# A two-layer transformer on one Trainium2 core: the experts' routing in program order, its rows by halves, the first gather inside the first expert

## The chip, the cores and the metric

One NeuronCore of a Trainium2 chip runs the kernel; the other seven idle. Its engines are TensorE (PE), VectorE (DVE), ScalarE (ACT), GpSimd (POOL) and SyncE (SP), each with an instruction queue of its own, and 16 DMA engines. The metric is the device time of one execution in microseconds, lower is better.

## The reference, cut to what matters

The model has two blocks of two layers on a sequence of 256 positions with 1024 features, batch 1. What the change touches is the last sublayer, a mixture of eight experts of which each position uses two:

```python
def _moe(h, w_router, w_gu, w_down):
    hf = h.reshape(B * S, D)
    probs = jax.nn.softmax((hf @ w_router).astype(jnp.float32), axis=-1)
    vals, idx = lax.top_k(probs, TOP_K)
    wts = vals / jnp.sum(vals, axis=-1, keepdims=True)
    combine = jnp.sum(jax.nn.one_hot(idx, N_EXPERTS, dtype=jnp.float32) * wts[..., None], axis=1)
    y = jnp.zeros_like(hf)
    for e in range(N_EXPERTS):
        y = y + combine[:, e:e + 1] * _swiglu(hf, w_gu[e], w_down[e])
    return y.reshape(B, S, D)
```

Here h is the normalized and modulated residual (rmsnorm(x) * (1 + scale) + shift), and _swiglu multiplies silu(gate) with up and projects back from 1792 to 1024.

## The kernel before, in words

The 256 positions stand as two halves t of 128 partitions. All of the model is float32: every matrix product is made of three TensorE passes over a high and a low part (hi, lo) of each operand. Weights are streamed by the class Stream: SyncE loads a raw tile, ScalarE casts it to whi (L98), VectorE subtracts to get wlo (L99), and six pairs of buffers hold what is split. Stream.next hands out the next pair and splits ahead until five are in hand; its argument hold leaves that many out. In out_proj, the last projection before the experts, hold grows towards the end (more=2), so that only one pair of the experts' weights is split when it ends. W.behind holds the next twelve splits back behind two given instructions.

Instructions are ordered on each engine by the framework's scheduler, which may run a later one first. Inside the context manager in_order(PE, SC, V) each instruction of TensorE, ScalarE and VectorE is tied to the one traced before it on its engine, so that these three run in program order. In the kernel before, only run() stands inside it: the experts. The routing ahead of it is left to the scheduler.

The routing, from L1212 on: route(t) (L1195) transposes a half of xres in two groups of four blocks, copies each to SBUF on ScalarE, and multiplies by the router's weights wr; eight rows of logits lie in PSUM, are copied to lgT (L1206), transposed back (L1236) and scaled by the norm rs[t] with a bias (L1237). The square root of the norm is ScalarE's (L507 in rsqrt). VectorE takes maximum and index (L1244, L1245), makes the one-hot sel of the two chosen experts (L1246 to L1250), and three small matmuls count each position's slot in its expert, posm (L1252 to L1255). Meanwhile norm_rows makes the modulated rows h (L551 on VectorE, L553 on GpSimd or VectorE), split into hr: the high part on ScalarE (L1261), the low part on GpSimd or VectorE (L1262). Then come the token weights w (L1267 to L1278), the largest count over (L1284), and the weights wj and the row numbers ij by which the experts' results are collected at the end (L1294 to L1303).

experts() makes gather(e0) for each pair of experts: four selection matrices Sm on VectorE (L1343), and eight steps block(c), each four matmuls of 256 columns (L1352) and two casts to xT on ScalarE (L1356). run() calls all eight blocks of the first pair ahead of the first expert, then goes through eight experts e, each in four quarters j of 448 columns, each quarter in eight pieces i: st.next, and six matmuls (L1467 to L1469). A quarter's gate half goes through Silu on ScalarE (L1471), its up half is multiplied on VectorE (L1474), and the quarter before is turned and multiplied by the down weights in the same stretch. For the later pairs the gather's steps are already dealt out one by one inside the pieces:

```python
            def run():
                steps = gather(0)
                for _ in range(KD):
                    steps.pop(0)()
```

Of the kernel before, what the change touches and what calls it, by code (L numbers as in the profile page):

```python
# [11 lines left out]
I32 = mybir.dt.int32  # L12
# [176 lines left out]
def model(ctx: ExitStack, tc: tile.TileContext, A, out, cap=128):  # L189
# [355 lines left out]
    def norm_rows(t, scale, shift=None, r=None):  # L545
# [8 lines left out]
        return h  # L554

# [636 lines left out]

    def route(t):
# [12 lines left out]
        V.tensor_copy(lgT[t], pr[0:8, 0:128])  # L1206
# [5 lines left out]
    with moe_ph as ph:  # L1212
        hr = [po.tile([128, 2, D], F32R, name=x) for x in ("oh", "ol")]
        unit = p.tile([128, 2, 144], F32R, name="unit")
        V.tensor_copy(unit[:, :, 0:128], ident[:, None, :].to_broadcast([128, 2, 128]))
        posm = p.tile([128, 2, 8], F32, name="posm")
        over = p.tile([128, 1], I32, name="over")
        slot = p.tile([128, 2, 128], F32, name="slot")
        for i in range(2):
            GP.iota(slot[:, i], pattern=[[1, 128]], base=i * cap + 1, channel_multiplier=0,  # L1220
                    allow_small_or_imprecise_dtypes=True)
            if cap < 128:
                GP.memset(slot[:, i, cap:], -5.0)
        p0 = p
        tri = p.tile([128, 128], F32R, name="tri")
        V.tensor_scalar(tri, jp, 0.0, None, op0=OP.is_gt)
        io8 = p.tile([128, 8], F32, name="io8")
        GP.iota(io8, pattern=[[1, 8]], base=0, channel_multiplier=0, allow_small_or_imprecise_dtypes=True)
        sel = p.tile([128, 2, 8], F32R, name="sel")
        lg = p.tile([128, 2, 8], F32, name="lg")  # L1230
        pl = pc()
        rs = []
        for t in range(2):
            route(t)
            rs.append(norm_r(t))
            PE.transpose(pl[:, t * 8:t * 8 + 8], lgT[t], ident[0:8, 0:8])  # L1236
            V.scalar_tensor_tensor(lg[:, t], pl[:, t * 8:t * 8 + 8], rs[t], bias8, op0=OP.mult, op1=OP.add)  # L1237
        warm(AF.Exp)
# [4 lines left out]
        for t in range(2):  # L1243
            V.max(top[:, t], lg[:, t])  # L1244
            V.max_index(ti[:, t], top[:, t], lg[:, t])  # L1245
        V.tensor_copy(tf, ti[:, :, 0:2])  # L1246
        oh = p.tile([128, 2, 2, 8], F32, name="oh2")
        V.tensor_tensor(oh, io8[:, None, None, :].to_broadcast([128, 2, 2, 8]),
                        tf[:, :, :, None].to_broadcast([128, 2, 2, 8]), OP.is_equal)
        V.tensor_add(sel, oh[:, :, 0], oh[:, :, 1])  # L1250
        ps = pc()
        PE.matmul(ps[:, 0:8], lhsT=tri, rhs=sel[:, 0], start=True, stop=True)  # L1252
        PE.matmul(ps[:, 8:16], lhsT=ones, rhs=sel[:, 0], start=True, stop=False)
        PE.matmul(ps[:, 8:16], lhsT=tri, rhs=sel[:, 1], start=False, stop=True)
        V.scalar_tensor_tensor(posm, ps[:, 0:16].rearrange("p (t e) -> p t e", t=2), 1.0, sel.bitcast(F32),  # L1255
                               op0=OP.add, op1=OP.mult)
        for t in range(2):
            h = norm_rows(t, *mo_rows, r=rs[t])
            for j in range(2):
                sl = slice(j * 512, (j + 1) * 512)  # L1260
                fs = SC.copy(hr[0][:, t, sl], h[:, sl])  # L1261
                fv = (GP if (t, j) in ((0, 0), (0, 1), (1, 1)) else V).tensor_sub(hr[1][:, t, sl], h[:, sl], hr[0][:, t, sl].bitcast(F32))  # L1262
        W.behind(fs, fv)

        pr = p.tile([128, 2, 8], F32, name="pr")
        sums = p.tile([128, 2], F32, name="sums")
        V.tensor_sub(pr, lg, b3(top[:, :, 0]))  # L1267
        SC.activation(pr, pr, AF.Exp)
        V.tensor_reduce(sums, pr, axis=AX.X, op=OP.add)
        V.reciprocal(sums, sums)  # L1270
        V.tensor_mul(pr, pr, b3(sums))
# [274 lines left out]
```

## Time and profile before

| | us |
|---|---|
| median of 3 runs | 1327.18 |
| lowest, highest | 1326.76, 1331.44 |
| the profiled execution's own time | 1326.26 |
| its span, first to last instruction | 1324.4 |
| TensorE busy | 1254.7 (95%) |
| VectorE busy | 1076.9 (81%) |
| ScalarE busy | 846.5 (64%) |
| GpSimd busy | 37.0 (3%) |

All other numbers come from that one execution. "Busy" adds up the intervals in which an engine had an instruction running; TensorE's weight loads (PEld) overlap its matmuls. The granted clock (PEclk) is a share of 2.4 GHz, so 1.00 is 2.4 GHz and 0.50 is 1.2 GHz. In a timeline, a row stands for one instruction or for neighbours of one kind (x8), with the start of the first and the time from there to the end of the last; in brackets stands how long the engine had been idle before, and what ended that.

### The profile page before, as it was taken

How to read it: one execution, taken by the hardware profiler on the slowest of the kernel's cores; microseconds unless marked ns; L12 is line 12 of the kernel's file. 1: busy time of each engine (PE TensorE's matmuls, PEld its weight loads, DVE VectorE, ACT ScalarE, POOL GpSimd, SP SyncE). 2: the span in 40 equal slices, each digit the busy share in tenths (PEclk: the TensorE clock that was granted, in tenths of full speed). 3: DMA queues.
4: the chain of work that ended last, by engine and by line, in shares of the span. 5: the costliest groups of instructions: out<-in, count | busy, mean ns of one | idle time of the engine just before them, and what ended most of it. 6: DMA issues, size and time to landing. Idle time of an engine off the chain costs nothing. (4 is left out here: it accounts for less than half of the span.)

```text
span 1324.4 us, 20099 instructions
## 1 busy us (share of the span) xinstructions
PE 1254.7 (95%) x7459; PEld 1118.0 (84%) x7459; DVE 1076.9 (81%) x1761; ACT 846.5 (64%) x1354; POOL 37.0 (3%) x68
## 2 busy tenths in 40 slices
PE   6988999999999989999998988999999999999985
PEld 6976989999798779999987667899999889988873
DVE  6796799997897496878768867988888898888976
ACT  7874456555566453434447747788778777878762
POOL 4000000000100000000000020000000000000100
PEclk9988999999899989999979998999999999999987
DMA  9844599892785287899642145999999999999980
GB/s 330 305 143 148 159 384 343 295 315 96 231 259 163 80 307 262 312 382 346 221 138 92 32 138 192 389 372 361 368 385 366 352 381 363 370 357 391 375 320 34
DMA packets 190171, 359.56 MB, mean 271 GB/s; under 512 B 15460, under 2 KB 147970, under 8 KB 189937
## 3 DMA queue, kind: packets, MB, share of 16 engines
q1 hardware_dynamic: 187361, 351.70, 75.1%
q10 hardware_dynamic: 1584, 3.91, 0.8%
q0 software_dynamic: 1120, 2.58, 0.5%
q8 instruction: 61, 1.00, 0.3%
q14 instruction: 45, 0.37, 0.1%
HBM read 351.56 MB, written 7.06 MB: 271 GB/s over the span
## 5 line engine op out<-in xcount | busy, mean ns | idle before, releaser
L99 DVE TENSOR_TENSOR wlo<-raw,whi 128x1024 fp32r<-128x1024 f32 (+2 forms) x577 | 644.5, 1155 | 126.0 <-ACT whi L98 119.0
L98 ACT CAST whi<-raw 128x1024 fp32r<-128x1024 f32 (+2 forms) x577 | 557.7, 1003 | 115.9 <-PE pa L489 30.8
L1467 PE MATMUL pa<-whi,xT 128*128 128x448 f32 x512 | 189.3, 370 | 3.8 <-ACT whi L98 3.8
L1468 PE MATMUL pa<-wlo,xT 128*128 128x448 f32 x512 | 187.0, 365 | 1.7 <-DVE wlo L99 1.7
L1469 PE MATMUL pa<-whi,xT 128*128 128x448 f32 x512 | 186.0, 363 | 0.0
L289 DVE SCALAR_TENSOR_TENSOR acc<-raw,cact,acc 128x1024 f32<-128x1024 f32 x84 | 107.2, 1276 | 2.9 <-DMA raw<-in_w_ada_dram 2.7
L1467 PEld LDWEIGHTS pa<-whi,xT 128*128 128x128 f32 x512 | 96.7, 189 | 11.9 <-ACT whi L98 4.9
L1468 PEld LDWEIGHTS pa<-wlo,xT 128*128 128x128 f32 x512 | 96.8, 189 | 9.4 <-DVE wlo L99 3.1
L1469 PEld LDWEIGHTS pa<-whi,xT 128*128 128x128 f32 x512 | 96.5, 189 | 6.4
L486 PE MATMUL pb<-whi,hTh 128*128 128x512 f32 x224 | 88.4, 395 | 0.7 <-ACT hTh L524 0.7
L487 PE MATMUL pb<-wlo,hTh 128*128 128x512 f32 x224 | 88.4, 395 | 0.1
L478 PE MATMUL pb<-hTh,whi 128*128 128x256 f32 x512 | 74.6, 289 | 1.1 <-ACT hTh L575 0.9
L478 PEld LDWEIGHTS pb<-hTh,whi 128*128 128x128 f32 x512 | 70.3, 196 | 6.0 <-ACT hTh L575 1.6
L478 PE MATMUL pb<-hTl,whi 128*128 128x256 f32 x512 | 72.4, 283 | 0.0
L478 PE MATMUL pb<-hTh,wlo 128*128 128x256 f32 x512 | 71.9, 283 | 0.0
L489 PE MATMUL pb<-whi,hTl 128*128 128x512 f32 x224 | 71.0, 395 | 0.0
L487 PE MATMUL pa<-wlo,fh 128*128 128x512 f32 x176 | 69.2, 393 | 0.6 <-DVE wlo L99 0.6
L486 PE MATMUL pa<-whi,fh 128*128 128x512 f32 x176 | 69.3, 394 | 0.0
L478 PEld LDWEIGHTS pb<-hTl,whi 128*128 128x128 f32 x512 | 66.3, 192 | 0.0
L478 PEld LDWEIGHTS pb<-hTh,wlo 128*128 128x128 f32 x512 | 66.1, 192 | 0.0
L478 PE MATMUL pc<-hTh,whi 128*128 128x256 f32 x448 | 63.8, 285 | 1.2 <-ACT whi L98 1.2
L478 PE MATMUL pc<-hTh,wlo 128*128 128x256 f32 x448 | 63.0, 283 | 0.0
(433 smaller groups left out, 2074.0 us busy)
## 6 DMA issues: line engine op xcount, KB each, us to landing
raw<-in_moe_w_gu_dram SPq DMA_DIRECT2D x128, 896.0 KB, 7.4
raw<-in_moe_w_down_dram SPq DMA_DIRECT2D x56, 1024.0 KB, 6.7
raw<-in_w_ada_dram SPq DMA_DIRECT2D x48, 1024.0 KB, 7.8
raw<-in_w_up_dram SPq DMA_DIRECT2D x22, 1024.0 KB, 9.7
raw<-in_ffn_w_gu_dram SPq DMA_DIRECT2D x22, 1024.0 KB, 6.2
raw<-in_na_w_qkv_dram SPq DMA_DIRECT2D x12, 1024.0 KB, 5.1
raw<-in_w_down_dram SPq DMA_DIRECT2D x11, 1024.0 KB, 4.8
raw<-in_ffn_w_down_dram SPq DMA_DIRECT2D x11, 1024.0 KB
```

What stands on the lines that cost most here:

```text
L98: self.last = self.nc.scalar.copy(h, src)
L99: self.nc.vector.tensor_sub(l, src, h.bitcast(F32))
L289: V.scalar_tensor_tensor(ada_acc[0], raw, cact[:, k:k + 1], ada_acc[0], op0=OP.mult, op1=OP.add)
L478: PE.matmul(ps, lhsT=w[:, k], rhs=x[:, k], start=n + k == 0, stop=n == 2 and k == KD - 1)
L486: PE.matmul(acc[t][j][:, :n], lhsT=xh, rhs=ws[j][0], start=first, stop=False)
L487: PE.matmul(acc[t][j][:, :n], lhsT=xh, rhs=ws[j][1], start=False, stop=False)
L489: PE.matmul(acc[t][j][:, :n], lhsT=xl, rhs=ws[j][0], start=False, stop=last)
L1467: PE.matmul(ps, lhsT=xh, rhs=wh, start=k == 0, stop=False)
L1468: PE.matmul(ps, lhsT=xh, rhs=wl, start=False, stop=False)
L1469: PE.matmul(ps, lhsT=xl, rhs=wh, start=False, stop=k == KD - 1)
```

## The change

The routing moves into run()'s program order: a new function routing(gather) issues it, given to experts as first. Its order is written out by hand: half 0's norm, router, first half row and logits, then half 1's, then the choice, then the other half rows. The rows are made by halves of 512 columns, row (two VectorE instructions), head (ScalarE) and rest (VectorE); GpSimd has no part in them any more, and W.behind goes. route(t) hands back its last copy so that routing can place it. keep_clock(n) issues n matmuls of 512 columns on constants. Only gather(0)'s four Sm are made in routing; its eight blocks are dealt out two by two to the first four pieces of the first expert, behind st.next. The token weights, over, wj and ij move to weigh(), which is called once, at the first piece of the first expert's second quarter (j = 1, i = 0). The switch of ScalarE's table to Exp ahead of the routing's end (warm) goes. The constants unit, tri, io8 and slot are issued ahead of out_proj. Cut to its core:

```diff
+
+    def keep_clock(n):
+
+        ps = pbc()
+        for _ in range(n):
+            tc.keep_in_program_order(PE.matmul(ps, lhsT=ones, rhs=ones[:, None, :].to_broadcast([128, 4, 128]),
+                                               start=True, stop=True))
...
+    unit = p.tile([128, 2, 144], F32R, name="unit")
+    V.tensor_copy(unit[:, :, 0:128], ident[:, None, :].to_broadcast([128, 2, 128]))
...
+    tri = p.tile([128, 128], F32R, name="tri")
+    V.tensor_scalar(tri, jp, 0.0, None, op0=OP.is_gt)
+    io8 = p.tile([128, 8], F32, name="io8")
+    GP.iota(io8, pattern=[[1, 8]], base=0, channel_multiplier=0, allow_small_or_imprecise_dtypes=True)
...
                 PE.matmul(pr[0:8, 0:128], lhsT=wr[:, k], rhs=xT[:, j], start=k == 0, stop=k == KD - 1)
-        V.tensor_copy(lgT[t], pr[0:8, 0:128])
+        return lambda: V.tensor_copy(lgT[t], pr[0:8, 0:128])
...
-        W.behind(fs, fv)
...
+        hx = [wk.tile([128, D], F32, name="h") for _ in range(2)]
+        pl = pc()
+        rs = []
+
+        def logits(t):
+            PE.transpose(pl[:, t * 8:t * 8 + 8], lgT[t], ident[0:8, 0:8])
...
+        def row(t, j):
+            sl = slice(j * 512, (j + 1) * 512)
+            V.scalar_tensor_tensor(hx[t][:, sl], xres[:, t, sl], rs[t], mo_rows[0][:, sl], op0=OP.mult, op1=OP.mult)
+            V.tensor_add(hx[t][:, sl], hx[t][:, sl], mo_rows[1][:, sl])
+        def head(t, j):
+            sl = slice(j * 512, (j + 1) * 512)
+            SC.copy(hr[0][:, t, sl], hx[t][:, sl])
+        def rest(t, j):
+            sl = slice(j * 512, (j + 1) * 512)
+            V.tensor_sub(hr[1][:, t, sl], hx[t][:, sl], hr[0][:, t, sl].bitcast(F32))
+        def choose():
+            V.tensor_copy(tf, ti[:, :, 0:2])
+            V.tensor_tensor(oh, io8[:, None, None, :].to_broadcast([128, 2, 2, 8]),
+                            tf[:, :, :, None].to_broadcast([128, 2, 2, 8]), OP.is_equal)
+            V.tensor_add(sel, oh[:, :, 0], oh[:, :, 1])
+            ps = pc()
+            PE.matmul(ps[:, 0:8], lhsT=tri, rhs=sel[:, 0], start=True, stop=True)
+            PE.matmul(ps[:, 8:16], lhsT=ones, rhs=sel[:, 0], start=True, stop=False)
+            PE.matmul(ps[:, 8:16], lhsT=tri, rhs=sel[:, 1], start=False, stop=True)
+            V.scalar_tensor_tensor(posm, ps[:, 0:16].rearrange("p (t e) -> p t e", t=2), 1.0, sel.bitcast(F32),
+                                   op0=OP.add, op1=OP.mult)
+        def weigh():
+            V.tensor_sub(pr, lg, b3(top[:, :, 0]))
+            SC.activation(pr, pr, AF.Exp)
+            V.tensor_reduce(sums, pr, axis=AX.X, op=OP.add)
+            V.reciprocal(sums, sums)
...
+            ps = pc()
+            for t in range(2):
+                PE.matmul(ps[:, 0:8], lhsT=ones, rhs=sel[:, t], start=t == 0, stop=t == 1)
+            V.tensor_reduce(cnt, ps[:, 0:8], axis=AX.X, op=OP.max)
+            V.tensor_copy(over, cnt)
+            tmp4 = ssx["junk"][:, 0:32].rearrange("p (t j e) -> p t j e", t=2, j=2)
...
+            V.tensor_mul(tmp4, oh, b4(w))
...
+            V.tensor_copy(ij, pj)
+        def routing(gather):
+
+            rs.append(norm_r(0))
+            copy = route(0)
+            row(0, 0)
+            copy()
+            logits(0)
+            row(0, 1)
+            rs.append(norm_r(1))
+            copy = route(1)
             for j in range(2):
+                head(0, j)
+            copy()
+            logits(1)
+            keep_clock(4)
+            choose()
+            row(1, 0)
+            head(1, 0)
+            steps = gather(0)
+            rest(0, 0)
+            rest(1, 0)
+            row(1, 1)
+            head(1, 1)
+            rest(0, 1)
+            rest(1, 1)
+            keep_clock(8)
+            return steps
 
...
             def run():
-                steps = gather(0)
-                for _ in range(KD):
-                    steps.pop(0)()
+                steps = first(gather) if first else gather(0)
                 prev, fin, when = None, None, {}
...
                             w = st.next(hold=2 if e == 7 and j == 3 and i > 4 else 0)
-                            if steps and i % 2 == 0:
+                            if e == j == 0 and i < 4:
                                 steps.pop(0)()
+                                steps.pop(0)()
+                            elif steps and i % 2 == 0:
+                                steps.pop(0)()
+                            if gate is not None and (e, j, i) == (0, 1, 0):
+                                weigh()
...
-        experts(W, slot[:, 0], last_gate)
+        experts(W, slot[:, 0], last_gate, first=routing)
```

## Rows read from the trace of the kernel before

**Rows 1.** Busy time by stretch: us, PE, PEld, DVE, ACT, POOL, clock, DMA share, GB/s

```profile
760.00:780.00 20.00, 20.00 (x97) 15.46 (x97) 7.09 (x14) 7.18 (x14) 0.65 (x3) 1.00 0.56 184
789.00:794.00 5.00, 0.28 (x2) 0.13 (x1) 4.93 (x8) 1.72 (x5) 3.40 (x3) 1.00 0.20 58
794.50:804.00 9.50, 5.82 (x23) 5.32 (x24) 5.54 (x33) 3.03 (x10) 1.29 (x1) 0.50 0.03 9
809.40:1255.00 445.60, 445.60 (x2225) 401.79 (x2226) 392.48 (x411) 360.14 (x464) 1.62 (x1) 1.00 1.02 370
```

**Rows 2.** TensorE's groups of instructions while the experts run: busy, mean | idle

```profile
L1467 PE MATMUL pa<-whi,xT 128*128 128x448 f32 x480 | 176.5, 368 | 0.4 <-ACT whi L98 0.4
```

**Rows 3.** Timeline of PE in the routing: start, us, engine, line, operation [idle before]

```profile
782.69 1.03 PE L1200 MATMUL pb<-ident,xres 128*128 128x128 f32 x8
783.96 1.92 PE L1205 MATMUL pc<-acc,wr 128*8 128x128 f32 x16 [0.24 <-ACT acc L1202]
...
792.19 0.22 PE L1236 MATMUL pc<-ident,shiftl 8*128 8x8 f32 x1 [3.14 <-DVE shiftl L1206]
796.96 0.38 PE L1252 MATMUL pc<-sel,tri 128*128 128x8 f32 x1 [4.55 <-DVE sel L1250]
...
799.41 0.93 PE L1352 MATMUL pc<-Sm,oh 128*128 128x256 f32 x2 [1.22 <-DVE unit L1277]
...
805.39 0.50 PE L1352 MATMUL pc<-Sm,oh 128*128 128x256 f32 x2 [0.27 <-ACT xT L1356]
...
806.50 0.36 PE L1467 MATMUL pa<-whi,xT 128*128 128x448 f32 x1
806.70 0.36 PE L1468 MATMUL pa<-wlo,xT 128*128 128x448 f32 x1
...
809.37 0.47 PE L1468 MATMUL pa<-wlo,xT 128*128 128x448 f32 x1 [0.65 <-DVE wlo L99]
```

**Rows 4.** Timeline of POOL in the routing

```profile
789.93 3.13 POOL L1262 TENSOR_TENSOR ol<-h,oh 128x512 fp32r<-128x512 f32 x2 [0.65 <-ACT oh L1261]
```

**Rows 5.** Timeline of DVE in the routing

```profile
785.26 0.75 DVE L551 SCALAR_TENSOR_TENSOR h<-xres,ry,bc 128x512 f32<-128x512 f32 x1
...
789.52 2.42 DVE L551 SCALAR_TENSOR_TENSOR h<-xres,ry,bc 128x512 f32<-128x512 f32 x2
...
793.53 0.21 DVE L1237 SCALAR_TENSOR_TENSOR lg<-pc,ry,bias 128x8 f32<-128x8 f32 x1
793.67 0.68 DVE L553 TENSOR_TENSOR h<-h,bc 128x512 f32<-128x512 f32 x1
...
796.75 0.16 DVE L1250 TENSOR_TENSOR sel<-oh 128x16 fp32r<-128x16 f32 x1
...
797.80 0.18 DVE L1255 SCALAR_TENSOR_TENSOR posm<-pc,sel 128x16 f32<-128x16 f32 x1 [0.57 <-PE pc L1254]
...
799.36 0.28 DVE L1343 TENSOR_SCALAR Sm<-slot,posm 128x128 fp32r<-128x128 f32 x1
...
800.96 0.17 DVE L1303 CAST ij<-junk 128x4 int32<-128x4 f32 x1
808.23 4.10 DVE L99 TENSOR_TENSOR wlo<-raw,whi 128x896 fp32r<-128x896 f32 x4 [7.10 <-ACT whi L98]
```

**Rows 6.** Timeline of ACT in the routing

```profile
783.33 1.07 ACT L1202 COPY acc<-pb 128x512 f32<-128x512 f32 x2 [1.02 <-PE pb L1200]
...
786.98 0.29 ACT L507 ACTIVATE ry<-ssx,re 128x1 f32<-128x1 f32 x1
...
804.69 1.20 ACT L1356 CAST xT<-pc 128x256 fp32r<-128x256 f32 x4 [0.42 <-PE pc L1352]
...
807.24 5.16 ACT L98 CAST whi<-raw 128x896 fp32r<-128x896 f32 x6
```

**Rows 7.** Timeline of all engines at the first expert's first quarters

```profile
813.25 1.28 ACT L1471 ACT_TABLE_LOAD   x1
...
819.97 0.61 DVE L1474 TENSOR_TENSOR hm<-hm,pa 128x448 f32<-128x448 f32 x1
```

More of the change, by code (lines that the diff above doesn't have):

```diff
@@ L1191, in model @@
     lgT = [sh.tile([KD, 128], F32, name="shift" + x) for x in "hl"]
+    unit = p.tile([128, 2, 144], F32R, name="unit")
+    V.tensor_copy(unit[:, :, 0:128], ident[:, None, :].to_broadcast([128, 2, 128]))
+    posm = p.tile([128, 2, 8], F32, name="posm")
+    over = p.tile([128, 1], I32, name="over")
+    slot = p.tile([128, 2, 128], F32, name="slot")
+    for i in range(2):
+        GP.iota(slot[:, i], pattern=[[1, 128]], base=i * cap + 1, channel_multiplier=0,
+                allow_small_or_imprecise_dtypes=True)
+        if cap < 128:
+            GP.memset(slot[:, i, cap:], -5.0)
+    tri = p.tile([128, 128], F32R, name="tri")
+    V.tensor_scalar(tri, jp, 0.0, None, op0=OP.is_gt)
+    io8 = p.tile([128, 8], F32, name="io8")
+    GP.iota(io8, pattern=[[1, 8]], base=0, channel_multiplier=0, allow_small_or_imprecise_dtypes=True)
     def route(t):
@@ L1213, in model @@
         hr = [po.tile([128, 2, D], F32R, name=x) for x in ("oh", "ol")]
[L1214 to L1228, printed above, removed]
         sel = p.tile([128, 2, 8], F32R, name="sel")
         lg = p.tile([128, 2, 8], F32, name="lg")
[L1231 to L1238, printed above, removed]
         b3 = lambda x, n=8: x[:, :, None].to_broadcast([128, 2, n])
@@ L1242, in model @@
         tf = p.tile([128, 2, 2], F32, name="tf")
-        for t in range(2):
+        oh = p.tile([128, 2, 2, 8], F32, name="oh2")
+        pr = p.tile([128, 2, 8], F32, name="pr")
+        sums = p.tile([128, 2], F32, name="sums")
+        w = p.tile([128, 2, 8], F32, name="w")
+        cnt = p.tile([128, 1], F32, name="cnt")
+        wj = p.tile([128, 2, 2], F32, name="wj")
+        ij = p.tile([128, 2, 2], I32, name="ij")
+        hx = [wk.tile([128, D], F32, name="h") for _ in range(2)]
+        pl = pc()
@@ L1250, in model @@
[L1250 to L1258, printed above, removed]
-            for j in range(2):
-                sl = slice(j * 512, (j + 1) * 512)
-                fs = SC.copy(hr[0][:, t, sl], h[:, sl])
-                fv = (GP if (t, j) in ((0, 0), (0, 1), (1, 1)) else V).tensor_sub(hr[1][:, t, sl], h[:, sl], hr[0][:, t, sl].bitcast(F32))
@@ L1263, in model @@
-        W.behind(fs, fv)
[L1265 to L1271, printed above, removed]
-        w = p.tile([128, 2, 8], F32, name="w")
-        V.tensor_mul(w, pr, sel.bitcast(F32))
-        V.tensor_reduce(sums, w, axis=AX.X, op=OP.add)
-        V.reciprocal(sums, sums)
@@ L1276, in model @@
-        V.tensor_mul(w, w, b3(sums))
-        V.tensor_copy(unit[:, :, 128:136], w)
-        V.tensor_sub(unit[:, :, 136:144], w, unit[:, :, 128:136].bitcast(F32))
-        ps = pc()
-        for t in range(2):
-            PE.matmul(ps[:, 0:8], lhsT=ones, rhs=sel[:, t], start=t == 0, stop=t == 1)
-        cnt = p.tile([128, 1], F32, name="cnt")
-        V.tensor_reduce(cnt, ps[:, 0:8], axis=AX.X, op=OP.max)
-        V.tensor_copy(over, cnt)
+        def row(t, j):
+            sl = slice(j * 512, (j + 1) * 512)
+            V.scalar_tensor_tensor(hx[t][:, sl], xres[:, t, sl], rs[t], mo_rows[0][:, sl], op0=OP.mult, op1=OP.mult)
+            V.tensor_add(hx[t][:, sl], hx[t][:, sl], mo_rows[1][:, sl])
@@ L1331, in collect, with experts @@
             return [[lambda t=t: first(t), lambda t=t: half(t, 0), lambda t=t: half(t, 1)] for t in range(2)]
-        def experts(st, slots, gate=None, yacc=None):
+        def experts(st, slots, gate=None, yacc=None, first=None):
             ex = {}
```

37 lines of the change are left out of this document (18 added, 19 removed).

## The prediction

> **What bounds the kernel now.** I read the busy time by stretch first. Up to the last projection TensorE is busy throughout at the full clock; from 809.4 to 1255 us, the eight experts, it is busy 445.60 of 445.60 us, again at 2.4 GHz; between them lies the routing, where it does 0.28 us in 5 [rows 1]. Next, what TensorE waits for inside the experts: its group of first products, 480 instructions, waited 0.4 us in all [rows 2]. So the experts are a block of TensorE work of fixed length, VectorE (392 us), ScalarE (360 us) and the DMA engines (share 1.02) close behind it but under it [rows 1]. A change to the routing moves the end by as much as it moves the moment from which TensorE runs without gaps, plus any new gap in the first expert.
>
> Then the timeline engine by engine. TensorE's chain before: transposes from 782.69, router products from 783.96, the second half's logits only at 792.19 (it waited for VectorE's copy), the slot counts at 796.96, the first gather block at 799.41, the first expert product at 806.50. Then a hole: only one weight tile had been split ahead, six products at a pitch of 0.20 use it up, and the eighth waited for wlo until 809.37. From there nothing stops it [rows 3]. The first expert's first four tiles (24 products) ended at about 809.37 + 16 x 0.20 for those behind it + 0.5 for its own start and the last one's tail = 813.1 us. That is the moment I carry forward.
>
> **The change, part by part.** The sum is made against the profiled execution's own 1326.26 us (span 1324.4); the median shown is 1327.18, 0.9 above it.
>
> *GpSimd leaves the rows.* While POOL ran two subtractions (3.13 us) [rows 4], VectorE's two row products took 2.42 together [rows 5]; alone one takes 0.75, so that pair lost 0.9 us. That is saved, and three subtractions and two additions of 0.68 come to VectorE instead [rows 5].
>
> *Program order in the routing.* The scheduler had run eight transposes in one go (1.03), then all sixteen router instructions (1.92) [rows 3]. In program order TensorE does four transposes (0.52), waits for ScalarE's copy (0.54 each [rows 6]), does eight router instructions (0.96), and all that once more: 0.52 + 0.54 + 0.96, twice, plus about 0.06 at each of eight hand-overs, is 4.5 us. For the first half: transposes from 782.69, products done at 787.2; ScalarE has out_proj's last square to do in between (some 0.6), so I take 787.7, and the copy to lgT (0.27) ends at 788.0. VectorE's row(0,0) (0.75 + 0.68 from 785.26 [rows 5]) is done by then and costs nothing. Then the transpose (0.22), logits, maximum and index (four small ones, about 0.75 with their gaps): 789.1. row(0,1): 790.5. Now the point where I chose: norm_r(1) comes before route(1) in program order, so ScalarE's square root (0.29 [rows 6]) waits for VectorE to finish row(0,1), and route(1)'s copies queue behind that root on ScalarE. Root done at 791.0; its transposes are long done, so the rest of route(1) is 0.54 + 0.96 + 0.52 + 0.54 + 0.96 + hand-overs = 3.8: 794.8; copy 795.1; transpose and logits 796.2; tf, oh, sel 0.6: 796.8. Before, sel ended at 796.75 + 0.16 = 796.9 [rows 5]. VectorE stands idle for some 3 us meanwhile. What the absence of GpSimd saves, the serial route of the second half takes back.
>
> *From the choice to the first product.* The counts take some 0.5 us at the full clock (797.80 - 796.96 = 0.84 at half [rows 3, 5]): posm at 797.6. Then VectorE in order: row(1,0) 1.4, four Sm at about 0.2 (0.28 with tail [rows 5]) 0.9, two subtractions 1.3: block 0 can start at 801.1, against 799.41. row(1,1) 1.4 and the copy of head(1,1) 0.54: 803.0. Behind head(1,1) on ScalarE stand, because st.next comes ahead of the gather's steps, four weight casts of 0.86 (5.16 / 6 [rows 6]): 806.4. Only then come the casts of xT for blocks 0 and 1 (1.20 for two blocks [rows 6]): 807.6, and TensorE waits for them; its product groups of k = 0 and 1 end at 808.3. Who waits for that: blocks 2 and 3, which follow them on TensorE.
>
> *The gather inside the pieces.* Each further pair: two blocks of four matmuls (about 0.46 each at the full clock, from the spacing behind 805.39 [rows 3]), the second block's casts behind the first's on ScalarE, the last three products: 0.46 + 1.20 + 0.17 + 0.60 = 2.43. Three pairs: 808.3 + 7.3 = 815.6, against 813.1: **2.5 us later**. The weight tiles are no wait any more (VectorE has wlo 1 to 4, 4.10 us [rows 5], by 808.0), which is the hole of before closed; it was only about 1.9 us.
>
> *The clock.* Before, it was still 1.00 five us into the pause and 0.50 from 794.5 to 804.0, although TensorE worked again from 799.41 on [rows 1, 3]. In the changed order TensorE has blocks 0 and 1 at 801 to 802 and then nothing until about 807.1, a pause like the one that cost the clock before; the eight dummy matmuls are issued right behind the counts (797.5 to 799.3), before that pause and not in it. I take the stretch at 1.2 GHz behind that pause to be as long as the one of before from 799.41 to 804.0, so from 807.0 to 811.5, in which some 4 us of work take twice what they would at 2.4 GHz: **2.0 us** more. The bounds: nothing (the casts hide it), and 4.
>
> *weigh().* 22 VectorE instructions of up to 0.19, one Exp, and two small matmuls move into the second quarter; they had filled gaps of the routing up to 800.96 [rows 5]. VectorE first owes the product hm (0.61 [rows 7]) and one split (4.10 / 4 = 1.03), then weigh 4.2 + 0.4 for Exp, then the next split: 7.2 us, while TensorE has five tiles ready, 5 x 1.2 = 6.0, and 0.4 of its own: **0.8 us** short. Below: 0, if the lead is larger; above: 2.1, if the table load (1.28 [rows 7]) stands in the chain. The Trainium skill (ScalarE: Activation LUTs, What ACT_TABLE_LOAD costs) speaks against this move: it gives about 2.66 us for a switch of table sets, load and drain together, and asks to batch functions by set. The row shows 1.28 for the load; with the figure of the Trainium skill the upper bound would be 3.5.
>
> *At nothing:* unit, tri, io8 and slot are issued earlier in the text, but their engines were free and the pool's memory, not the text, sets when they run. The SyncE queue: weight loads are issued when a split frees a raw tile; the first now comes some 4 us earlier, and no TensorE wait inside the experts hangs on it [rows 2]. The end phase is unchanged.
>
> Sum: 2.5 + 2.0 + 0.8 = 5.3, so 1326.26 + 5.3 = **1331.5 us**. About 0.5%, 6.6 us, is what a measurement of this kernel can tell from no change; this lies inside it.
>
> **Rivals.**
> *The clock falls in the routing already* (slower). In the new order TensorE works less than half the time from 785 on. For it: the router's copies now stand between its bursts. Against: before, 0.28 us in 5 were still granted the full clock [rows 1]. If it falls by 792, route(1)'s sixteen router instructions go from 0.12 to 0.24, its transposes and the counts double too: 1.9 + 0.4 + 0.3 = 2.6 more, on the chain: 1334.1. It decides if the granted clock is 0.50 before 792.
> *No wait behind the root* (faster). If ScalarE's and TensorE's parts of route(1) run under row(0,1), as the scheduler had them, sel comes 3.4 earlier, and the pause of TensorE with it: 1331.5 - 3.4 = 1328.1, and 1326.1 if the clock then holds. Against it: the order is forced on all three engines.
> *Exp's table load in VectorE's chain*: ScalarE's load begins only after the wait for pr: 1332.8. With the switch that the Trainium skill gives (ScalarE: Activation LUTs, What ACT_TABLE_LOAD costs) it would be 1334.2.
> *The change doesn't do what it says*: the whole gather is anyway paced by ScalarE's casts, TensorE's order in the first expert is as good as before, and wlo's hole and the new waits cancel: 1327.
>
> **How the numbers follow.** Chances: my forecast 0.47, clock in the routing 0.25, no wait behind the root 0.13, table load 0.07, no effect 0.08. The range: down to 1325.5 (the faster rival with the clock held), up to 1336.5 (the clock rival with the upper bound of weigh or of the clock's cost). Faster than 1320.5 needs more than any saving found here: 0.04. Slower than 1333.8: two thirds of the clock rival, half of the table rival, a fifth of the forecast's own spread: 0.17 + 0.035 + 0.095 = 0.30. The rest, 0.66, is no change.
>
> **What would show it.** Right: sel on VectorE near 796.8; VectorE idle for some 3 us before the second copy to lgT; four casts of whi between head(1,1) and the first xT; TensorE idle from about 802 to 807, the clock 0.50 behind it; the first four tiles done near 817. Wrong: if sel is before 794, or the first xT is cast before whi, or the gaps are as said but TensorE waits again for weights in the middle of the experts.

## The result, and the profile after

| | before | after |
|---|---|---|
| median of 8 runs, us | 1326.97 | 1335.65 |
| lowest, highest | 1325.61, 1331.44 | 1334.07, 1342.19 |
| ratio, 95% interval | | 1.0067 [1.0051, 1.0082] |
| the profiled execution's time | 1326.26 | 1336.25 |
| its span | 1324.4 | 1334.2 |

The change costs 8.7 us, and the interval of the ratio lies clear of 1. The time lies in the range of the prediction (1325.5 to 1336.5), 4.2 us above its likeliest value, and in the case "Slower than 1333.8", which had 0.30 against 0.66 for no change.

The two profiled executions differ by 9.8 us, but 1.4 of that is older than the change: TensorE's first transpose of the router starts at 784.06 instead of 782.69 [rows 3], behind code that differs only in the constants issued early. Over all executions shown below this moment, from here on **T0**, moves between 782.7 and 789.6, and between 784.1 and 789.6 over those whose code up to there is the changed kernel's; so whether the early constants have a part in the 1.4 can't be seen. Every stage is therefore told from T0, and the part of the change behind T0 is 550.1 - 541.7 = 8.4 us from T0 to the end.

Busy time by stretch in the changed kernel (us, PE, PEld, DVE, ACT, POOL, clock, DMA share, GB/s), beside [rows 1]:

```profile
784.00:789.00 5.00, 3.33 (x25) 2.05 (x23) 4.04 (x8) 2.50 (x6) 0.00 (x0) 1.00 0.26 105
789.00:794.00 5.00, 2.12 (x13) 1.41 (x13) 3.13 (x13) 0.77 (x2) 0.00 (x0) 0.75 0.00 0
794.00:799.00 5.00, 3.90 (x17) 2.10 (x16) 0.38 (x2) 1.62 (x3) 0.00 (x0) 0.50 0.00 0
...
834.00:1264.00 430.00, 429.89 (x2146) 387.20 (x2147) 378.99 (x398) 345.82 (x447) 0.29 (x1) 1.00 1.01 369
```

The experts are the same block of TensorE work as before (429.89 of 430.00 us). The loss lies ahead of them: the clock falls in the second stretch already, and in 794 to 799 VectorE does 0.38 us of work and ScalarE 1.62. The timeline of TensorE, which answers to [rows 3]:

```profile
784.06 0.60 PE L1222 MATMUL pb<-ident,xres 128*128 128x128 f32 x4
785.33 1.04 PE L1227 MATMUL pc<-acc,wr 128*8 128x128 f32 x8 [0.68 <-ACT acc L1224]
...
792.69 1.88 PE L1227 MATMUL pc<-acc,wr 128*8 128x128 f32 x8 [2.51 <-ACT acc L1224]
794.50 1.12 PE L1222 MATMUL pb<-ident,xres 128*128 128x128 f32 x4
796.34 1.88 PE L1227 MATMUL pc<-acc,wr 128*8 128x128 f32 x8 [0.73 <-ACT acc L1224]
...
801.16 3.76 PE L560 MATMUL pc<-ones 128*128 128x512 f32 x8
804.72 0.62 PE L1397 MATMUL pc<-Sm,oh 128*128 128x256 f32 x2
...
810.61 0.74 PE L1515 MATMUL pa<-whi,xT 128*128 128x448 f32 x1 [4.57 <-ACT xT L1401]
...
834.11 0.47 PE L1516 MATMUL pa<-wlo,xT 128*128 128x448 f32 x1 [1.26 <-DVE wlo L99]
```

Three waits stand out: 2.51 us for a copy of the router, 4.57 for the first xT, 1.26 for wlo in the second quarter. Behind the first, eight router products take 1.88 us; eight of the first half, at 785.33, took 1.04. ScalarE shows what the first two waited for, and where Exp's table went:

```profile
791.87 0.29 ACT L507 ACTIVATE ry<-ssx,re 128x1 f32<-128x1 f32 x1 [3.96 <-DVE re L505]
792.07 0.57 ACT L1224 COPY acc<-pb 128x512 f32<-128x512 f32 x1
...
806.31 0.62 ACT L1267 CAST oh<-h 128x512 fp32r<-128x512 f32 x1 [2.76 <-DVE h L1263]
806.84 3.45 ACT L98 CAST whi<-raw 128x896 fp32r<-128x896 f32 x4
810.20 1.18 ACT L1401 CAST xT<-pc 128x256 fp32r<-128x256 f32 x4
...
826.62 1.28 ACT L1290 ACT_TABLE_LOAD   x1
829.02 0.22 ACT L1290 ACTIVATE pr<-pr 128x16 f32<-128x16 f32 x1 [1.12 <-DVE pr L1289]
...
831.77 1.28 ACT L1519 ACT_TABLE_LOAD   x1
833.06 0.55 ACT L1519 ACTIVATE hm<-pa 128x448 f32<-128x448 f32 x1
```

And VectorE, beside [rows 5]:

```profile
798.26 0.28 DVE L1228 COPY shiftl<-pc 8x128 f32<-8x128 f32 x1 [5.45 <-PE pc L1227]
...
800.14 0.17 DVE L1278 TENSOR_TENSOR sel<-oh 128x16 fp32r<-128x16 f32 x1
801.34 0.18 DVE L1283 SCALAR_TENSOR_TENSOR posm<-pc,sel 128x16 f32<-128x16 f32 x1 [1.02 <-PE pc L1282]
...
828.82 0.17 DVE L1289 TENSOR_TENSOR pr<-lg,top 128x16 f32<-128x16 f32 x1
...
832.89 0.17 DVE L1317 CAST ij<-junk 128x4 int32<-128x4 f32 x1
832.97 2.08 DVE L99 TENSOR_TENSOR wlo<-raw,whi 128x896 fp32r<-128x896 f32 x2
```

The order is what the prediction described: the square root behind VectorE's rows with the copy right behind it, VectorE idle ahead of the second copy to lgT, four casts of whi between the last head and the first xT, weigh() as one block of 4.2 us (828.82 to 832.97) ahead of the next split.

### The profile page after: what moved, and what is told of

Its sections match the earlier page's. It is cut to its first block, busy times and chain, and to the rows that moved or that the text cites. A ratio compares the mean times of both kernels' runs of the same rounds, so it can differ in the third digit from the quotient of the medians.

```text
span 1334.2 us, 20116 instructions
## 1 busy us (share of the span) xinstructions
PE 1262.4 (95%) x7471; PEld 1122.0 (84%) x7471; DVE 1078.4 (81%) x1766; ACT 847.9 (64%) x1354; POOL 29.2 (2%) x63
## 5 line engine op out<-in xcount | busy, mean ns | idle before, releaser
L98 ACT CAST whi<-raw 128x1024 fp32r<-128x1024 f32 (+2 forms) x577 | 558.0, 1003 | 115.5 <-PE pa L489 32.4
L1515 PEld LDWEIGHTS pa<-whi,xT 128*128 128x128 f32 x512 | 97.0, 190 | 16.2 <-ACT xT L1401 5.2
```

The lines of the kernel that those rows point to most:

```text
L98: self.last = self.nc.scalar.copy(h, src)
L1515: PE.matmul(ps, lhsT=xh, rhs=wh, start=k == 0, stop=False)
```

## The experiments

All stages, in us from T0, read from each kernel's timeline: end of posm, start of the first and of the 24th product of the first expert, then from the 24th product to the end, and from T0 to the end. The ratio is that of the timed runs to the kernel before on the same chip; on the three chips of the experiments the kernel before took 1330.5, 1331.1 and 1329.9 us in the median, on the first one 1327.0. Each row of stages comes from one profiled execution.

| kernel | posm | product 1 | product 24 | 24 to end | T0 to end | ratio [95%] |
|---|---|---|---|---|---|---|
| before | 15.3 | 23.8 | 30.0 | 511.7 | 541.7 | 1 |
| after | 17.5 | 26.6 | 36.9 | 513.3 | 550.1 | 1.0067 [1.0051, 1.0082] |
| x1 gather ahead of splits | 16.1 | 21.9 | 32.3 | 514.0 | 546.3 | 1.0027 [1.0014, 1.0041] |
| x2 root behind router | 13.0 | 22.1 | 32.9 | 513.3 | 546.2 | 1.0041 [1.0024, 1.0059] |
| x3 weigh in piece 1 | 14.9 | 24.0 | 35.2 | 511.6 | 546.7 | 1.0080 [1.0051, 1.0109] |
| x4 waits filled | 14.9 | 24.0 | 32.4 | 512.4 | 544.7 | 1.0030 [1.0017, 1.0044] |
| y3 no constant products | 17.3 | 26.4 | 36.8 | 513.2 | 549.9 | 1.0050 [1.0031, 1.0069] |
| y1 only GpSimd out | 11.8 | 20.6 | 26.7 | 511.8 | 538.5 | 0.9969 [0.9952, 0.9986] |
| y2 only gather in pieces | 15.3 | 18.6 | 28.6 | 510.8 | 539.4 | 0.9987 [0.9972, 1.0002] |
| w1 both of these | 11.8 | 16.1 | 25.5 | 510.8 | 536.2 | 0.9971 [0.9957, 0.9985] |
| z1 casts early | 13.0 | 17.3 | 25.7 | 513.1 | 538.9 | 0.9982 [0.9969, 0.9995] |
| z2 and router interleaved | 9.3 | 13.5 | 23.4 | 512.0 | 535.4 | 0.9953 [0.9934, 0.9972] |
| z3 and casts ahead of heads | 9.3 | 15.0 | 22.9 | 511.1 | 534.0 | 0.9962 [0.9947, 0.9976] |
| z4 without constant products | 9.3 | 15.9 | 23.7 | 511.7 | 535.3 | 0.9954 [0.9938, 0.9970] |

**Parts of the changed kernel undone.** x1 puts the gather's blocks ahead of the weight stream in the first four pieces:

```diff
-                            w = st.next(hold=...)
                             if e == j == 0 and i < 4:
                                 steps.pop(0)()
                                 steps.pop(0)()
+                            w = st.next(hold=...)
```

> The changed kernel with one edit: in the first four pieces of the first expert the two gather blocks are issued ahead of st.next, so that ScalarE casts xT of blocks 0 and 1 before the four weight casts. My theory (ScalarE's program order holds the first product): the first xT cast starts about 3.4 us sooner after block 0, the first product some 3 to 4 us sooner; xT of blocks 2 and 3 still stand behind the four casts, so 2 to 3 us of it reach the end: 1332.7 to 1333.7 against the changed kernel's 1335.7. Rival (the first pieces are held by the wlo tiles, not by xT): no change, 1335.7.

ScalarE of this run, at the same place:

```profile
808.33 0.62 ACT L1267 CAST oh<-h 128x512 fp32r<-128x512 f32 x1 [2.76 <-DVE h L1263]
808.85 1.19 ACT L1401 CAST xT<-pc 128x256 fp32r<-128x256 f32 x4
809.90 3.49 ACT L98 CAST whi<-raw 128x896 fp32r<-128x896 f32 x4
813.27 1.22 ACT L1401 CAST xT<-pc 128x256 fp32r<-128x256 f32 x4
```

xT now follows the head at once. From posm to the 24th product it takes 32.3 - 16.1 = 16.2 us, against 19.4 after: 3.2 are back, the shorter pause's clock included. Of the four casts a part is still in the way, ahead of the second pair of blocks, and the wait for wlo in the second quarter grows from 1.26 to 2.11, so 2.5 of the 3.2 reach the end, as expected; the other 1.3 of the 3.8 from T0 to the end come from the clock in the routing (see the last section).

x2 takes away the wait of route(1) behind the square root:

```diff
-            rs.append(norm_r(1))
             copy = route(1)
+            rs.append(norm_r(1))
```

> The changed kernel with norm_r(1) issued behind route(1) instead of ahead of it, so that ScalarE's router copies of the second half no longer queue behind the square root. My theory (the root makes the serial route of half 1 wait for row(0,1)): sel on VectorE ends 2 to 3.5 us sooner, VectorE's hole ahead of the second lgT copy shrinks from 5.5 to 2 to 3 us, and if the router then runs at 2.4 GHz another 1 to 2: total 1331 to 1333.5. Rival (the route's length on TensorE alone, at 1.2 GHz, is the bound, the root stands beside it): under 1 us, 1335.

sel ends at T0 + 12.2, against 16.3 after and 14.1 where the changed order keeps its clock (x3, x4): the wait alone costs 1.9, and with it goes the 2.51 us pause of TensorE, around which the clock had fallen; here it is 1.00 until 805, ahead of the first product. What follows is that the place of one VectorE group ahead of ScalarE's root cost 1.9 us at the full clock and 4.0 in the execution profiled. In the timed runs x2 and the changed kernel are not clearly apart (1.0041 and 1.0067, the intervals overlapping).

x3 moves weigh() from the second quarter to the first expert's second piece, ahead of the blocks:

```diff
-                            if gate is not None and (e, j, i) == (0, 1, 0):
-                                weigh()
...
+                            if gate is not None and (e, j, i) == (0, 0, 1):
+                                weigh()
                             if e == j == 0 and i < 4:
```

> The changed kernel with weigh() called in the second piece of the first expert (e, j, i = 0, 0, 1), right behind st.next and ahead of the gather blocks, where the trace of the changed kernel shows VectorE idle for 3.1 and ScalarE for 1.9 us. My theory (weigh in the second quarter makes TensorE wait 1.3 us for wlo): that wait is gone and so is one of the two extra table loads: 1.3 to 1.7 us less, 1334.0 to 1334.4. Rival (the wait at the second quarter is the small lead after the routing, not weigh): the wait stays, and Exp ahead of the xT casts costs 1 more: 1336.5.

The wait for wlo in the second quarter is gone, and with it 1.7 us behind the 24th product (511.6 against 513.3, before 511.7). But 0.9 is lost between posm and the 24th product (20.3 against 19.4 after). ScalarE and TensorE there:

```profile
815.66 0.22 ACT L1290 ACTIVATE pr<-pr 128x16 f32<-128x16 f32 x1
816.66 0.65 ACT L1401 CAST xT<-pc 128x256 fp32r<-128x256 f32 x2 [0.78 <-PE pc L1397]
...
817.36 0.51 PE L1397 MATMUL pc<-Sm,oh 128*128 128x256 f32 x2 [0.74 <-ACT xT L1401]
```

Exp, which the rival blamed, is not what costs it: ScalarE is through with it and waits 0.78 us for block 2. It is block 3 that TensorE can start only when block 2's casts are done, 0.74 us later. The blocks and weigh()'s two small products share two PSUM buffers (pc), and weigh() seems to hold one of them; that is read from the kernel, no run isolates it.

From T0 to the end this execution is 3.4 us shorter than that of the changed kernel, 2.6 of it at posm, where its clock held (see the last section). In the timed runs nothing of it is left: 1.0080 from four runs, the changed kernel's 1.0067 from eight, the intervals overlapping. Whether the place is better as a whole stays open; that the wait for wlo belongs to weigh() is shown.

x4 adds products on constants inside TensorE's waits (3, 4, 11 and 3 behind the router's groups, 18 behind the first two blocks):

```diff
             SC.copy(xT, ps.rearrange("p (j n) -> p j n", j=4))
+            fill(((3, 4), (11, 3))[t][b])
...
                                 steps.pop(0)()
+                                if i == 0:
+                                    fill(18)
```

> The changed kernel with further dummy matmuls of 512 columns where TensorE waits: 3 and 4 in route(0), 11 and 3 in route(1), 18 behind the first two gather blocks. They hold up nothing by their own length if the clock is 2.4 GHz (0.22 each). My theory (1.2 GHz in the routing and in the first pieces costs some 4.5 us): the granted clock stays at 1.00 from 784 to 820, the two router bursts of half 1 take 1.0 instead of 1.9 us each, the first product groups 0.6 instead of 1.1: 4 to 5 us less, 1331 to 1332. Rival (the stage is paced by VectorE's and ScalarE's queues, the clock is beside the path): clock at 1.00 all the same, but under 1.5 us: 1334.5 or more.

posm comes at 14.9, 2.6 earlier than after (x3 had that without the fillings), and from there the 24th product takes 17.5, 1.9 less than after and 2.8 less than x3, 0.9 of which x3 had lost to weigh(). So 1.9 is what the clock behind the casts had cost. The clock is 1.00 from T0 to 44 us behind it, the stretch of the casts ahead of xT among them (busy time by stretch), where it was at 0.50 for a time in all five executions of these orders without fillings (after, x1, x2, x3, y3):

```profile
809.00:814.00 5.00, 4.28 (x19) 3.27 (x18) 4.76 (x7) 4.77 (x9) 0.00 (x0) 1.00 0.44 132
```

Another 0.9 us is gained behind the 24th product; what brings it is not shown. y3, the opposite, takes out the products that the change had brought:

```diff
-            keep_clock(4)
...
-            keep_clock(8)
```

> The changed kernel without its 4 and 8 products on constants. My theory: they lie in stretches where TensorE waits anyway and not in the pause that lowers the clock, so they hold nothing: the 24th product at T0 + 35 to 37.5 (with them 36.9 in the changed kernel's profile, 35.2 in one execution whose routing kept its clock), time within 1.5 us of the changed kernel. Rival (they keep the clock over part of the way): the clock at 0.50 over 2 us or more longer, 24th product at T0 + 38 or later, time 2 us or more above the changed kernel. Rival (they are in the way: counts and first block queue behind them at half clock): 24th product 1.5 us or more earlier.

Nothing moves (36.8 against 36.9, T0 to the end 549.9 against 550.1). They do touch the clock: with them it is back at 1.00 from T0 + 21.8 to T0 + 24.2 (805.9 to 808.3), without them it stays at 0.50 from T0 + 7.4 to T0 + 31.2 (792.2 to 816.0 in y3). But those 2.4 us lie in the wait for xT, where TensorE has 0.14 us of work. So where the change put them they bring nothing and don't stand in the way; in the waits of x4 the clock held.

**Parts of the change alone, in the kernel before.** y1 gives GpSimd's five half rows to VectorE and leaves the order to the scheduler:

```diff
-                (GP if (t, j) in ((0, 0), (0, 1)) else V).tensor_add(h[:, sl], h[:, sl], shift[:, sl])
+                V.tensor_add(h[:, sl], h[:, sl], shift[:, sl])
...
-                fv = (GP if (t, j) in ((0, 0), (0, 1), (1, 1)) else V).tensor_sub(...)
+                fv = V.tensor_sub(...)
```

> The kernel before, with GpSimd's two additions and three subtractions given to VectorE and nothing else changed (the scheduler still orders the routing). My theory: the part without GpSimd is no loss and no gain of note: the pair of row products takes 1.5 instead of 2.4 us, but five half rows of 0.68 come to VectorE, so sel at T0 + 14 to 16 (before 14.2), the 24th product at T0 + 29.5 to 31.5 (before 30.0), and the time within 1.5 us of the kernel before. Rival (GpSimd hid work that VectorE now pays in full): 24th product over 2 us later, time 2 to 3.5 us above before. Rival (the shared work was what held VectorE back): 24th product 1.5 us or more earlier.

I was wrong and the second rival was right: posm 3.5 earlier, the 24th product 3.3, the time 0.31% down. GpSimd in the kernel before, its two stretches beyond [rows 4]:

```profile
786.09 3.18 POOL L553 TENSOR_TENSOR h<-h,bc 128x512 f32<-128x512 f32 x2 [20.36 <-DVE h L551]
...
795.07 1.29 POOL L1262 TENSOR_TENSOR ol<-h,oh 128x512 fp32r<-128x512 f32 x1 [2.01 <-DVE ol L1262]
```

VectorE of the same execution:

```profile
787.46 0.61 DVE L509 SCALAR_TENSOR_TENSOR rq<-ssx,ru 128x1 f32<-128x1 f32 x1
...
788.14 1.15 DVE L513 SCALAR_TENSOR_TENSOR ru<-ry,rq 128x1 f32<-128x1 f32 x1
...
792.06 1.54 DVE L553 TENSOR_TENSOR h<-h,bc 128x512 f32<-128x512 f32 x1
...
795.19 1.19 DVE L1246 CAST tf<-ti 128x4 f32<-128x4 uint32 x1
```

The same four instructions in y1, where GpSimd is idle:

```profile
793.26 0.14 DVE L509 SCALAR_TENSOR_TENSOR rq<-ssx,ru 128x1 f32<-128x1 f32 x1
...
793.98 0.21 DVE L513 SCALAR_TENSOR_TENSOR ru<-ry,rq 128x1 f32<-128x1 f32 x1
...
794.25 0.67 DVE L553 TENSOR_TENSOR h<-h,bc 128x512 f32<-128x512 f32 x1
...
797.92 0.15 DVE L1246 CAST tf<-ti 128x4 f32<-128x4 uint32 x1
```

In the kernel before they lose 0.47, 0.94, 0.87 and 1.04 us, and the pair of [rows 5] another 0.96 (2.42 - 2 x 0.73): 4.3 us. Each lies beside a GpSimd instruction, and two end with it: 788.14 + 1.15 = 789.29 with 786.09 + 3.18 = 789.27, and 795.19 + 1.19 = 796.38 with 795.07 + 1.29 = 796.36. Taken singly, GpSimd's five instructions end at 788.05, 789.27, 791.39, 793.06 and 796.36, and each of these ends has one stretched VectorE instruction beside it: the three short ones end 0.02 us later (788.07, 789.29, 796.38), the two of 128x512 0.55 us later (791.94, 793.61). Not every overlap costs: the row product of 786.19 keeps its 0.73 us beside GpSimd's first instruction, which takes 1.96. Of the 4.3 us 3.2 arrive at sel, since VectorE now has six 128x512 instructions in place of three between the second copy to lgT and sel.

y2 deals the first gather into the pieces and changes nothing else:

```diff
                 steps = gather(0)
-                for _ in range(KD):
-                    steps.pop(0)()
...
-                            if steps and i % 2 == 0:
+                            if e == j == 0 and i < 4:
+                                steps.pop(0)()
+                                steps.pop(0)()
+                            elif steps and i % 2 == 0:
                                 steps.pop(0)()
```

> The kernel before, with the first gather's eight blocks dealt two by two into the first four pieces, behind the weight stream, and nothing else changed: the routing stays with the scheduler, GpSimd and the token weights stay where they were. My theory: the dealing alone is no loss, since the hole of before (TensorE waiting for wlo until 809.37) closes: first product near T0 + 20 (before 23.8) with the first xT pushed back by the weight casts by 1 to 2 us, three pairs of blocks at 2.4 us each, the 24th product at T0 + 27 to 30 (before 30.0), time 0 to 3 us below before. Rival (the dealing is what costs, as the casts ahead of xT did behind the forced order): first xT 3 us or more later than before, at T0 + 21 or later, 24th product at T0 + 31.5 or later, time 1.5 us or more above before.

As expected: 1.4 us earlier at the 24th product; the timed runs (0.9987) don't tell it from no change. Here the casts of whi do no harm: the scheduler has the heads done early, and ScalarE does four casts while it waits for the first block. Its timeline in y2:

```profile
800.54 0.93 ACT L98 CAST whi<-raw 128x896 fp32r<-128x896 f32 x1
801.38 0.21 ACT L1268 ACTIVATE pr<-pr 128x16 f32<-128x16 f32 x1
801.50 2.60 ACT L98 CAST whi<-raw 128x896 fp32r<-128x896 f32 x3
806.35 0.65 ACT L1356 CAST xT<-pc 128x256 fp32r<-128x256 f32 x2 [2.24 <-PE pc L1352]
```

w1 is the sum of the two edits.

> The two parts of the change that were each no loss alone, together in the kernel before: GpSimd out of the rows (24th product 3.3 us earlier alone) and the first gather dealt two by two into the first pieces (1.5 us earlier alone). The routing stays with the scheduler, the token weights stay in it, there are no products on constants. My theory (the forced order, not these two parts, is what costs): both add up, posm at T0 + 11.5 to 12.5, 24th product at T0 + 24.5 to 26.5, end at T0 + 536 to 538, 3 to 5.5 us faster than before, where the whole change is 8 us slower. Rival (both close the same hole, TensorE's wait for wlo): the end at T0 + 538.5 or later, no better than with GpSimd out alone.

In the profiled executions they add up: 4.5 earlier at the 24th product (3.3 + 1.4 expected), 5.5 from T0 to the end. The timed runs show w1 0.29% faster than the kernel before, but no better than y1 alone (0.31%, on another chip). So two parts of the change, without its order, are a gain; the order written out by hand and weigh() turn it into a loss.

**Better orders.** z1 keeps the program order and mends what the runs above had found. `W.early(4)` casts the high parts of four weight tiles where ScalarE waits, `W.late` subtracts their low parts later; weigh() hands back twelve groups, one in every second piece:

```diff
-            rs.append(norm_r(1))
             copy = route(1)
+            rs.append(norm_r(1))
...
+            W.early(4)
             choose()
...
             rest(1, 0)
+            for _ in range(2):
+                steps.pop(0)()
+            W.late(1)
             row(1, 1)
...
             rest(1, 1)
-            keep_clock(8)
+            W.late(3)
```

(keep_clock(8) now follows choose(), and blocks 2 to 7 follow the products of pieces 0 to 2.)

> The changed kernel with four edits of order: the second half's root behind its router; the high parts of the next four weight tiles cast on ScalarE while it waits in the routing, their low parts subtracted behind the first rests; two blocks ahead of the last rows, the other six behind the products of pieces 0 to 2; the token weights in twelve small groups over quarters 2 to 4. If my account of the loss is right (casts ahead of xT, the pause that they make and the clock behind it, the token weights in one go), posm is at T0 + 13, the first product at T0 + 17 to 19 (after 26.6), the 24th at T0 + 25 to 27.5 (after 36.9, before 30.0), no wait for wlo in the second quarter, and the end at T0 + 537 to 540 (before 541.7): 2 to 4 us faster than the kernel before. Rival (the clock falls in the routing whatever stands behind it, since TensorE works there half the time at most): 24th product at T0 + 29 or later, time within 1.5 us of before or above.

The stages come within the ranges expected: product 24 at 25.7, 11.1 earlier than after, with the clock at 1.00 from T0 to 44 us behind it, so the rival does not show. Behind it the groups of weigh() still cost 1.4 (513.1 against 511.7). z2 also interleaves the halves' router on TensorE (turn is a group's transposes and copy, mul its products) and makes row(0, 1) behind the choice:

```diff
-            copy = route(0)
+            turn(0, 0)
+            turn(0, 1)
+            mul(0, 0, pr0)
+            turn(1, 0)
+            mul(0, 1, pr0)
             row(0, 0)
...
+            turn(1, 1)
             logits(0)
+            mul(1, 0, pr1)
+            mul(1, 1, pr1)
```

> As the run before, and the two halves' router interleaved on TensorE (transposes of a group ahead of the products of the one before), the second half rows of both halves behind the choice. My theory: what the forced order lost in the routing is the serial chain of the two halves; interleaved, sel is at T0 + 9 to 10.5 (after 16.3, before 14.2), posm at T0 + 10 to 11.5, the first product at T0 + 15 to 17, the 24th at T0 + 22.5 to 25.5, the end at T0 + 533 to 537: 5 to 8 us faster than before. Rival (VectorE, which now owes all rows, rests and low parts in one stretch, takes the place of the chain): 24th product no more than 1 us earlier than in the run before, TensorE waiting for VectorE's ol or wlo in between.

sel ends at 8.5, earlier than expected, and the whole is 0.47% faster than before. Of the 3.7 us gained at posm 2.3 reach the 24th product. The one larger wait between is in part what the rival said: two heads, which wait for VectorE's rows, stand ahead of the casts of blocks 2 and 3. TensorE's timeline there:

```profile
805.23 0.47 PE L1551 MATMUL pa<-whi,xT 128*128 128x448 f32 x1 [1.44 <-ACT xT L1438]
```

z3 moves those two blocks ahead of the rows and weigh()'s groups into the third expert; z4 is z3 without keep_clock.

```diff
-            for _ in range(2):
+            for _ in range(4):
                 steps.pop(0)()
...
-                            if gate is not None and e == 0 and j > 0 and i % 2 == 0 and parts:
+                            if gate is not None and e == 2 and i % 2 == 1 and parts:
```

> As the interleaved run before, with two edits: blocks 2 and 3 of the gather ahead of the last rows, so that their casts on ScalarE do not queue behind the two heads (TensorE waited 1.44 us there), and the token weights in small groups inside the third expert in place of the first. Theory: 24th product at T0 + 22 to 22.7 (before this edit 23.4), from the 48th product to the end 506.5 to 507.0 (before this edit 507.2), end at T0 + 533.5 to 534.8: 7 to 8 us faster than the kernel before. Rival (VectorE's rests are the bound behind it): TensorE waits for ol ahead of block 4 by as much as it gains, end at T0 + 535 to 536.

> As the run before it, without the 4 and 8 products on constants. Here they lie inside the two waits of a TensorE that otherwise works. Theory: without them it is busy some 1.1 us in the 5 between the router and the first block, which is a pause like the one of the kernel before; the clock falls to 0.50 behind it for up to 5 us and the 24th product comes 1.5 to 3 us later than in the run before. Rival (the constants' products hold nothing, here as in the changed kernel): 24th product within 0.5 us.

z3 gains 0.5 at the 24th product, not 0.7 to 1.4: block 4 now waits for head and rest, as the rival said. weigh() in the third expert costs nothing any more (511.1). z4's clock falls, z3's does not, in the stretch of the first blocks. z3 (1.00 also in 797.66 to 802.66, which counted from T0 is the stretch shown of z4):

```profile
795.00:800.00 5.00, 3.88 (x17) 2.37 (x15) 4.21 (x14) 2.60 (x4) 0.00 (x0) 1.00 0.00 0
```

and z4:

```profile
795.00:800.00 5.00, 3.94 (x14) 3.27 (x15) 4.97 (x11) 1.99 (x6) 0.00 (x0) 0.53 0.05 10
```

It costs 0.8 at the 24th product, less than the 1.5 I had as the least. VectorE, busy 4.97 of these 5 us with either clock, seems to set the pace there; in the timed runs (0.9954 against 0.9962) it can't be seen. In the timed runs z2, z3 and z4 are 5 to 6 us, 0.4 to 0.5%, faster than the kernel before.

## Why the prediction was right in its range and low in its value

**The block of the experts and the mark of the 24th product**: right. All of the loss is at that mark (36.9 - 30.0 = 6.9) and at weigh() behind it. "From there nothing stops it" left out one place late in the experts, outside [rows 1]: TensorE waits 4.4 us for weights there (3.41 of it ahead of 1270.47), as ScalarE stands before an instruction that waits 3.83 us for a DMA. After the change it is 4.3, so it has no part in the loss.

**Program order in the routing, and from the choice to the first product**: right in sum. The forecast had, from T0, sel at 14.1, posm at 14.9 and the first xT at 23.7. Where the changed order keeps its clock (x3) these are 14.1, 14.9 and 23.6. Each further pair of blocks takes 2.43 to 2.44 at the full clock (x4), forecast 2.43. The four casts ahead of xT, the pause of TensorE and the clock behind it came as said: 810.61 to 814.72 takes 4.11 us for six products and two blocks, which at the full clock's pitches, 0.20 for a product and 0.24 for two of a block, would be 6 x 0.20 + 4 x 0.24 = 2.2: 1.9 lost, forecast 2.0. In all these steps had 4.5, and 6.9 less the rival below is 4.3; x3, whose clock held in the routing, gives the same: 35.2, less the 0.9 of weigh(), less 30.0.

**GpSimd leaves the rows**: the wrong size. I priced the contention at 0.9, from one pair of VectorE instructions [rows 5]; y1 shows 4.3 us of stretched instructions and 3.2 gained at sel. Only one of GpSimd's three stretches stood in my rows, and VectorE's short instructions, where most of it hides, I had not compared with themselves elsewhere. The Trainium skill (SBUF — State Buffer, Terms) has VectorE and GpSimd share a pair of ports that one of them holds for a full instruction while the other "fully blocks"; the five ends above agree with that. The time came out all the same, because sel was added up forward from its parts and not as before plus a difference. But the sentence "What the absence of GpSimd saves, the serial route of the second half takes back" hid 3 us of gain and 3 of loss, and that gain is w1.

**The clock falls in the routing already**: a rival with 0.25, and it is what the profiled execution did. Granted 0.87 in 790.06 to 792.06 and 0.50 behind it, posm at 17.5 instead of 14.9: 2.6, the price worked out. My reason against it, that TensorE had been granted the full clock at 0.28 us in 5, was too thin: it was one stretch of one execution, in another order of work. This is the step that failed, as a choice between cases; the case was there. How many of the eight timed executions had this fall is not known, and x3, whose profiled one had not, is no faster in its timed runs; so 2.6 is the price in the execution profiled.

**weigh()**: low. Forecast 0.8, bounds 0 and 2.1; measured 1.6 from the 24th product to the end. Of it 1.26 is the wait for wlo; some 0.2 of the rest is the two small products, which the forecast had counted as 0.4 of cover for TensorE and not as time on the engine that sets the end. The rival of Exp's table in VectorE's chain fell: the load runs at 826.62, before VectorE has pr (828.82), and VectorE then waits 0.28 for Exp. For the switch of sets, the Trainium skill's 2.66 us (ScalarE: Activation LUTs, What ACT_TABLE_LOAD costs) does not show here: the load of 831.77 takes 1.28 and the next function starts at 833.06.

**The dummy products do nothing**: right for the time (y3). **No wait behind the root** fell by the rows (2.51, 3.96); x2 shows what it would have brought, 1.9 at sel at the full clock, where the rival had 3.4.

Sum: 4.3 + 2.6 + 1.6 = 8.5, for 8.4 measured from T0 to the end (the first two are parts of the measured 6.9), where the forecast had 4.5 + 0 + 0.8. Most of what it missed is the clock in the routing.

## What to carry to other kernels

Before an order is written out by hand, write down for each queue which instruction waits at its head and what stands behind it that another engine needs: here one root behind a row, four weight casts ahead of xT and a block of small instructions between two splits cost more than two good parts of the same change had saved. Test such a change part by part, since the parts had opposite signs. And price contention from all of an engine's instructions that overlap the other one, the short ones first.

## What the runs showed of the hardware that was not expected

The clock of TensorE is not settled by the program alone. x1, x3, y3 and the changed kernel run the same instructions up to the second router group of the second half, with the same wait of 2.51 us. Stretches of 2 us from T0 + 6 on, in the changed kernel:

```profile
790.06:792.06 2.00, 0.12 (x2) 0.00 (x0) 1.80 (x7) 0.19 (x1) 0.00 (x0) 0.87 0.00 0
792.06:794.06 2.00, 1.37 (x7) 0.92 (x8) 0.66 (x4) 0.58 (x2) 0.00 (x0) 0.50 0.00 0
```

in x1:

```profile
793.39:795.39 2.00, 0.13 (x2) 0.00 (x0) 1.81 (x7) 0.18 (x1) 0.00 (x0) 1.00 0.00 0
795.39:797.39 2.00, 1.36 (x7) 0.89 (x8) 0.67 (x4) 0.58 (x2) 0.00 (x0) 0.56 0.00 0
797.39:799.39 2.00, 1.55 (x7) 0.73 (x5) 0.00 (x0) 0.35 (x1) 0.00 (x0) 0.59 0.00 0
```

and in x3:

```profile
794.77:796.77 2.00, 0.15 (x2) 0.00 (x0) 1.82 (x7) 0.17 (x1) 0.00 (x0) 1.00 0.00 0
796.77:798.77 2.00, 1.34 (x11) 1.01 (x12) 0.66 (x4) 0.60 (x2) 0.00 (x0) 1.00 0.00 0
```

The clock falls a little before the end of the wait and stays at half for 14 us, or it stays at half for under 4 us, or it does not fall, and posm ends at 17.5, 16.1 or 14.9; y3 went like the changed kernel (0.50 from 792.2 on, posm at 17.3). What decides between them no run here shows. A pause of such a length is therefore a risk of up to 2.6 us in this order, not a cost that one trace can give, and in none of the six executions without it (x2, x4, z1 to z4) did the clock fall ahead of posm.
